# Half-height and half-width matmuls of the attention and scan products issued in pairs, on one Trainium2 core

## Chip, core and metric

The kernel runs on one core of a Trainium2 chip. The metric is the device time of one execution in microseconds (us). Products run on TensorE (PE; its weight loads are listed as PEld), elementwise work on VectorE (DVE), ScalarE (ACT) and GpSimd (POOL), and SyncE (SP) issues the transfers from HBM.

## What is computed

The reference chains three layers for 256 tokens of width 1024. The first has a context of 256 more tokens and mixes tokens in three ways: differential attention, a gated linear scan and neighbourhood attention. The other two are alike: latent attention (MLA), stick-breaking attention and a pooling mixer. Each layer ends in a mixture of 32 experts. Cut to what the change touches:

```python
# first layer: differential attention, 4 heads, two 64-wide score maps per head, values 128 wide
s = einsum('bqhmd,bkhmd->bhmqk', qb, kb) * 64 ** -0.5
p = softmax(s); d = p[:, :, 0] - lam * p[:, :, 1]; o = einsum('bhqk,bkhv->bqhv', d, vb)
# first layer: gated scan, 4 heads, 32-wide keys, 64-wide values, chunks of 64 tokens, both directions
o = einsum('bhts,bhsv->bhtv', a_intra, vc) + einsum('bhtd,bhdv->bhtv', qc * exp(b), s)
# first layer: neighbourhood attention, 4 heads of 64, keys of the grid and of the context
# second and third layer: MLA, 8 heads, 96-wide scores, 64-wide values; stick-breaking, 4 heads of 64
a = where(strict, exp(log_sigmoid(z) + between), 0); o = einsum('bhqk,bkhd->bqhd', a, v)
# each layer: out = x + mix @ w_out, then the experts
```

## The kernel before

One program does the three layers in order: `first_phase`, `moe_phase`, and twice `second_phase` with `moe_phase`. Weights come from HBM in units of 1 MB through a ring of 22 buffers in SBUF: a list of transfers in a fixed order, each issued by SP as soon as a buffer is released. All matmuls are on fp32 data except the projections and gathers, which use a high and a low fp32r part (`mm3`, L561). An fp32 matmul stands in the trace as two instructions (two passes) with a weight load each, so counts below are twice the number of calls.

The order of the engines' work is written by hand. In `first_phase` the scan's pieces lie between projections of the attention operands, in the order of `SEQ_A`: capital letters are projections, `k` is `g_kj` (64-row products of keys and values), `s` `g_state`, `t` `g_step` (chunk state times query, L1189), `i` `g_intra` (32-row scores of one head, L1176), `p` `g_pv` (64-column value products of one head, L1203). Two PSUM banks (`tr`) serve these, two more (`po`) collect the scan's output.

Attention runs as items in `run_items`, one item a step, four steps deep. At step s PE gets the scores of item s (DVE and ACT then do its softmax), the transposes of item s-2 (`fin`, followed by an ACT copy out of PSUM), a filler (projection, modulation, output product) and last the value product of item s-3. In the first layer there are eight differential items (two scores each, L1301) and eight neighbourhood items (one score, L1327). The second and third layers have 12 items in the order `ITEMS_B`: M for MLA (scores L2127, transposes L2148), S for stick-breaking (scores L2162 and L2163, a running sum in `fin`, L2180 to L2182). Their value products `pv` (L2114, L2116) fill 64 output rows for an even head and the other 64 for an odd one. A step's length is PE's own work, unless the softmax of an item isn't through.

Where a head uses only 64 of the 128 contraction rows (differential and neighbourhood scores, stick-breaking scores), the query was stored twice with the other 64 rows set to zero, and the matmul ran over all 128 rows:

```python
qaT = [bq.t[:, i * 1024:(i + 1) * 1024].rearrange("p (a t) -> p a t", a=4) for i in range(2)]
pool.memset(qaT[0][64:128], 0.0)
pool.memset(qaT[1][0:64], 0.0)
```

Of the kernel before, what the change touches and what calls it, by code (L numbers as in the profile page):

```python
# [27 lines left out]
SEQ_A = "A k0 B s0 s1 C k1 t0 D i1 E i2 t1 F i3 t2 p1 G i0 p2 p0 H t3 p3"  # L28
# [344 lines left out]
def hybrid_kernel(ctx: ExitStack, tc: tile.TileContext, A, out, dbg=None):  # L373
# [388 lines left out]
    def run_items(items, fillers, mode):  # L762
        n = len(items)
        for s in range(max(n + 3, len(fillers))):
            if mode and 2 <= s < n + 2:
                items[s - 2][2]()
            if s < n:
                items[s][0]()
                items[s][1]()
            if 2 <= s < n + 2:  # L770
                items[s - 2][3]()
            if not mode and 1 <= s <= n:
                items[s - 1][2]()
            if s < len(fillers):
                fillers[s]()
            if 3 <= s < n + 3:
                items[s - 3][4]()

    def first_phase():
        with ExitStack() as es:  # L780
# [321 lines left out]
            qaT = [bq.t[:, i * 1024:(i + 1) * 1024].rearrange("p (a t) -> p a t", a=4) for i in range(2)]  # L1102
            pool.memset(qaT[0][64:128], 0.0)
            pool.memset(qaT[1][0:64], 0.0)
# [3 lines left out]
            def rope(dsts, src, n, cs, sn):  # L1108
# [6 lines left out]
                m = 128 // len(dsts)  # L1115
                for i, d in enumerate(dsts):
                    hs = slice(m * i, m * i + m)
                    dve.tensor_add(d[hs], src[hs], sw[hs, 0:n])

            def ka_sink(i):  # L1120
                st = Unit()

                def sink(f, p):
# [4 lines left out]
                    if f == 1:  # L1128
                        rope([kaT[:, 2 * i:2 * i + 2, 0:256]], st.kr, 2, cosv, sinv)
                return sink  # L1130

            def qa_sink(i):
                def sink(f, p):
                    kr = wg.tile([128, 2, 256], F32, name="kr")
                    act.activation(kr.rearrange("p a t -> p (a t)"), p, AF.Copy, scale=0.125)
                    rope([q[:, 2 * i:2 * i + 2] for q in qaT], kr, 2, cosv, sinv)
# [14 lines left out]
            def g_kj(d):  # L1151
                names = ["kbT", "qbT", "kbt", "glT"]
                for par in range(2):
                    js = [j for j in ((0, 1, 2) if d == 0 else (1, 2, 3)) if j % 2 == par]
                    p = bank(ps, "tr")
                    for i, j in enumerate(js):
                        pe.matmul(p[:, i * 256:(i + 1) * 256], lhsT=k2[64 * par:64 * par + 64, d, j // 2],
                                  rhs=vbt[64 * par:64 * par + 64, j // 2], start=True, stop=True)
# [10 lines left out]
            def g_intra(h):  # L1169
                at[h] = quarters[0][h].rearrange("p (z f) -> p z f", z=4)  # L1170
                pool.memset(at[h], 0.0)
                pa = bank(ps, "tr")
                for a in range(2):
                    for d in range(2):
                        z = 2 * a + d
                        pe.matmul(pa[:, z * 128:(z + 1) * 128],  # L1176
                                  lhsT=k3[32 * h:32 * h + 32, d, a * 128:(a + 1) * 128],
                                  rhs=q3[32 * h:32 * h + 32, d, a * 128:(a + 1) * 128], start=True, stop=True)
                for a in range(2):
                    dve.copy_predicated(at[h][:, 2 * a:2 * a + 2], mfb,  # L1180
                                        pa[:, a * 256:(a + 1) * 256].rearrange("p (d t) -> p d t", d=2))
# [17 lines left out]
            def g_pv(h):  # L1199
                pr, o = h // 2, 64 * (h % 2)  # L1200
                for a in range(2):
                    for d in range(2):
                        pe.matmul(og[pr][o:o + 64, a * 128:(a + 1) * 128], lhsT=vbt[:, a, h * 64:(h + 1) * 64],  # L1203
                                  rhs=at[h][:, 2 * a + d], start=False, stop=(a == 1 and d == 1),
                                  skip_group_check=True)
# [35 lines left out]
            qnT = [wd.tile([128, 2, 256], F32, name=f"qnT{i}") for i in range(2)]  # L1241
            S.release(c1u)
            pool.memset(qnT[0][64:128], 0.0)
            pool.memset(qnT[1][0:64], 0.0)
# [4 lines left out]
            def values(h, dT, vals, w, kind):  # L1249
                hp, odd = h // 2, h % 2  # L1250
                if odd == 0:
                    hold.po = bank(ps, "po")
                po = hold.po
                o = po[:, odd * 256:odd * 256 + 256] if kind == "d" else po[64 * odd:64 * odd + 64, 0:256]
                for kt in range(4):
                    pe.matmul(o, lhsT=vals[:, kt, h * w:(h + 1) * w], rhs=dT[:, kt], start=(kt == 0), stop=(kt == 3))
                if odd == 0:
                    return
                if kind == "n":
                    act.activation(mixT[:, 6 + hp], po[:, 0:256], AF.Copy)  # L1260
# [60 lines left out]
            def near_item(h, qt):  # L1321
# [67 lines left out]
            def qn_sink(f, p):  # L1389
                for i in range(2):  # L1390
                    hs = slice(64 * i, 64 * i + 64)
                    act.activation(qnT[i].rearrange("p a t -> p (a t)")[hs], p[hs], AF.Copy, scale=0.125)
# [882 lines left out]
```

## Time and profile before

| | us |
|---|---|
| median of 3 runs (1385.88 to 1387.04) | 1386.26 |
| the profiled execution | 1387.48 |
| its span, first to last instruction | 1385.7 |
| PE busy in it | 1233.4 |
| DVE, ACT, POOL busy | 433.9, 342.9, 98.3 |
| mean granted clock of TensorE, share of 2.4 GHz | 0.958 |

Busy shares are means over stages with different limits. In the expert stages transfers run at 420 GB/s nearly throughout; in the mixing stages PE is busy nearly throughout and the transfers pause.

### The profile page before, as it was taken

The numbers are of one execution on the slowest core, as the hardware profiler recorded it, in microseconds if no ns is written. First come the engines' busy times: TensorE is split into PE (matmuls) and PEld (weight loads), VectorE is DVE, ScalarE is ACT, GpSimd is POOL, SyncE is SP. The second block draws the span as 40 slices with busy tenths as digits, with TensorE's granted clock in tenths as the row PEclk, the third lists the DMA queues.
The fourth block names the chain that finished last, engine by engine and source line by source line (L and its number), as shares of the span: only waits on it lengthen the run. The fifth ranks groups of instructions, "written<-read, shape, count | busy, mean of one in ns | idle before, by whom it ended". The sixth has DMA issues, their size and how long they took to land. (4 is left out here: it accounts for less than half of the span.)

```text
span 1385.7 us, 18830 instructions
## 1 busy us (share of the span) xinstructions
PE 1233.4 (89%) x7278; PEld 671.4 (48%) x7278; DVE 433.9 (31%) x1024; ACT 342.9 (25%) x709; POOL 98.3 (7%) x87
## 2 busy tenths in 40 slices
PE   5999999999976799998779998998778999999776
PEld 3788875464221154442258764443227866444222
DVE  5456362352111021221165434221005534422102
ACT  4432252221000010110146522211105642212102
POOL 1354100000000000000012100000000210000000
PEclk9999999999999899999899999999999999999998
DMA  9644417859999999999993548999999365899996
GB/s 360 220 180 167 183 61 313 359 207 394 420 422 421 421 421 422 421 420 420 421 413 133 203 173 339 421 421 420 421 420 375 122 273 196 349 420 421 421 421 246
DMA packets 64537, 459.40 MB, mean 332 GB/s; under 512 B 7408, under 2 KB 7728, under 8 KB 9904
## 3 DMA queue, kind: packets, MB, share of 16 engines
q1 hardware_dynamic: 64432, 458.04, 81.1%
q8 instruction: 62, 1.02, 0.3%
q14 instruction: 43, 0.35, 0.1%
HBM read 466.40 MB, written 1.05 MB: 337 GB/s over the span
## 5 line engine op out<-in xcount | busy, mean ns | idle before, releaser
L1696 PE MATMUL up<-ring,xg 128*32 128x512 f32 (+2 forms) x2016 | 381.5, 646 | 61.0 <-DMA ring<-in_gu_dram 33.3
L1696 PEld LDWEIGHTS up<-ring,xg 128*32 128x32 f32 (+2 forms) x2016 | 106.2, 127 | 305.8 <-issue 190.1
L1696 PE MATMUL mm<-ring,hdT 128*32 128x512 f32 (+2 forms) x1008 | 186.9, 620 | 27.0 <-DMA ring<-in_dn_dram 22.6
L561 PE MATMUL ps<-ring,ring 128*128 128x256 f32 (+1 forms) x960 | 146.6, 311 | 1.2 <-POOL ring L894 0.6
L561 PEld LDWEIGHTS ps<-ring,ring 128*128 128x128 f32 x960 | 131.3, 196 | 20.0 <-issue 5.8
L1712 DVE TENSOR_TENSOR hd<-hd,up 128x256 f32<-128x256 f32 (+1 forms) x32 | 16.7, 521 | 381.4 <-ACT hd L1711 359.1
L1696 PEld LDWEIGHTS mm<-ring,hdT 128*32 128x32 f32 (+2 forms) x1008 | 53.7, 124 | 138.8 <-issue 90.5
L1711 ACT ACTIVATE hd<-up 128x256 f32<-128x256 f32 (+1 forms) x32 | 14.9, 465 | 386.8 <-PE up L1696 386.8
L1512 PEld LDWEIGHTS mm<-P,ring 128*128 128x128 f32 x512 | 67.0, 200 | 12.0 <-issue 10.3
L1512 PE MATMUL mm<-P,ring 128*128 128x256 f32 x512 | 71.1, 296 | 0.6 <-DVE xg L1522 0.3
L596 PE MATMUL mm<-ring,ring 128*128 128x512 f32 (+1 forms) x192 | 64.1, 487 | 0.0
L1742 DVE SCALAR_TENSOR_TENSOR yl<-mm,gt,yh 128x512 fp32r<-128x512 f32 x40 | 30.0, 751 | 96.0 <-ACT yh L1741 96.0
L1741 ACT ACTIVATE yh<-mm,gt 128x512 fp32r<-128x512 f32 x40 | 27.5, 688 | 98.8 <-PE mm L1696 98.8
L1736 DVE SCALAR_TENSOR_TENSOR mm<-mm,gt,gmod 128x512 f32<-128x512 f32 x24 | 18.2, 759 | 98.3 <-PE mm L1696 98.3
L1738 ACT ACTIVATE yh<-mm 128x512 fp32r<-128x512 f32 x24 | 14.3, 597 | 139.1 <-DVE mm L1736 139.1
L1989 PE MATMUL ps<-ring,ring 128*128 128x256 f32 x384 | 48.7, 286 | 0.0
L1989 PEld LDWEIGHTS ps<-ring,ring 128*128 128x128 f32 x384 | 47.1, 192 | 0.7 <-ACT ring L1968 0.4
L596 PEld LDWEIGHTS mm<-ring,ring 128*128 128x128 f32 x192 | 35.8, 190 | 23.7 <-issue 21.5
L1958 POOL TENSOR_SCALAR ring<-ring,fr 128x1024 f32<-128x1024 f32 x2 | 5.7, 2852 | 420.2 <-DMA ring<-in_win_dram 420.2
L820 POOL TENSOR_TENSOR ring<-ring,ring 128x1024 fp32r<-128x1024 f32 x12 | 30.2, 2513 | 49.0 <-ACT ring L819 38.2
L1942 DVE TENSOR_TENSOR ring<-ring,ring 128x1024 fp32r<-128x1024 f32 x24 | 28.1, 1221 | 14.1 <-ACT ring L1938 14.0
L1750 PE MATMUL po<-yh,sm 128*128 128x512 f32 x64 | 28.4, 444 | 1.6 <-ACT yh L1738 1.4
(464 smaller groups left out, 1385.6 us busy)
## 6 DMA issues: line engine op xcount, KB each, us to landing
ring<-in_gu_dram SPq DMA_DIRECT2D x128, 1024.0 KB, 19.7
ring<-in_dn_dram SPq DMA_DIRECT2D x124, 1024.0 KB, 19.7
ring<-in_up_dram SPq DMA_DIRECT2D x120, 1024.0 KB, 19.2
ring<-in_wmod_dram SPq DMA_DIRECT2D x24, 1024.0 KB, 5.1
ring<-in_win_dram SPq DMA_DIRECT2D x24, 1024.0 KB, 11.3
ring<-in_wout_dram SPq DMA_DIRECT2D x12, 1024.0 KB, 18.3
ring<-in_c_dram SPq DMA_DIRECT2D x2, 896.0 KB, 14.0
ring<-in_wsm_dram SPq DMA_DIRECT2D x2, 784.0 KB, 14.5
```

Source lines behind the costliest of these rows:

```text
L561: pe.matmul(out, lhsT=a, rhs=b, start=first and i == 0, stop=last and i == 2, skip_group_check=True)
L596: pe.matmul(po, lhsT=O.mixT[:, s, a * 128:(a + 1) * 128], rhs=O.w[2 * c + s // 4][:, s % 4, sl.start - 512 * c:sl.stop - 512 * c], start=( ...
L820: (pool if q else dve).tensor_sub(lo[:, sl], u.t[:, sl], hi[:, sl].bitcast(F32))
L1512: pe.matmul(o, lhsT=xx[:, a, dt * 128:(dt + 1) * 128], rhs=P[:, a], start=(k == 0), stop=(k == 3))
L1696: pe.matmul(out[w * e:w * e + w], lhsT=x_of(w * e, w * e + w), rhs=wt, start=start, stop=stop)
L1712: dve.tensor_mul(hd, hd, pu[:, hid:uw])
L1736: dve.scalar_tensor_tensor(pd, pd, s.gt, gmod[:, hf * 512:(hf + 1) * 512], op0=OP.mult, op1=OP.mult)
L1741: act.activation(yh, pd, AF.Copy, scale=s.gt)
L1742: dve.scalar_tensor_tensor(yl, pd, s.gt, yh.bitcast(F32), op0=OP.mult, op1=OP.subtract)
L1750: pe.matmul(y[2 * a + hf], lhsT=s.sm[:, a * 128:(a + 1) * 128], rhs=s.y[hf][i], start=False, stop=True, skip_group_check=True)
L1942: dve.tensor_sub(lo[:, sl], u.t[:, sl], hi[:, sl])
L1989: pe.matmul(p[:, f * 256:(f + 1) * 256], lhsT=w[pw][:, dt, f * 128:(f + 1) * 128], rhs=hT[ph][:, dt], start=(i == 0 and f == 0 and dt == 0 ...
```

## The change

Scores with 64 contraction rows now run on the upper or the lower 64 rows alone, two of them one after the other in program order, one on either half; the zero halves, their memsets and the second copies go. `g_intra` takes two heads at once (row groups 32 and 64, then 96 and 0), `g_step` uses the half of the state that isn't zero, `g_pv` alternates two heads on the two column halves. The neighbourhood and MLA and stick-breaking value products of an even head wait for the odd one, and both are issued alternately. Neighbourhood and stick-breaking scores of an odd head are issued with those of the even one, a step earlier. Neighbourhood items are reordered so that the heads of a pair follow each other. In `run_items` the value products of item s-3 move from the end of the step to before the transposes of item s-2 and the filler. Core of the diff:

```diff
-SEQ_A = "A k0 B s0 s1 C k1 t0 D i1 E i2 t1 F i3 t2 p1 G i0 p2 p0 H t3 p3"
+SEQ_A = "A k0 B s0 s1 C k1 t0 D i0 E t1 F i1 t2 G p0 H t3 p1"
...
             if s < n:
                 items[s][0]()
                 items[s][1]()
+            if 3 <= s < n + 3:
+                items[s - 3][4]()
             if 2 <= s < n + 2:
                 items[s - 2][3]()
             if not mode and 1 <= s <= n:
                 items[s - 1][2]()
             if s < len(fillers):
                 fillers[s]()
-            if 3 <= s < n + 3:
-                items[s - 3][4]()
...
-            def rope(dsts, src, n, cs, sn):
+            def rope(dst, src, n, cs, sn):
...
-                for i, d in enumerate(dsts):
-                    hs = slice(m * i, m * i + m)
-                    dve.tensor_add(d[hs], src[hs], sw[hs, 0:n])
+                dve.tensor_add(dst, src, sw[:, 0:n])
...
-            def g_intra(h):
+            def g_intra(i):
+                hs = (1, 2) if i == 0 else (3, 0)
...
+                        for h, pa in zip(hs, pas):
+                            pe.matmul(pa[:, z * 128:(z + 1) * 128],
+                                      lhsT=k3[32 * h:32 * h + 32, d, a * 128:(a + 1) * 128],
+                                      rhs=q3[32 * h:32 * h + 32, d, a * 128:(a + 1) * 128], start=True, stop=True)
...
-                        pe.matmul(og[pr][:, j * 64:(j + 1) * 64], lhsT=st[d][:, pr * 128:(pr + 1) * 128],
-                                  rhs=q1[:, d, j * 64:(j + 1) * 64], start=first[pr], stop=False,
+                        hs = slice(64 * pr, 64 * pr + 64)
+                        pe.matmul(og[pr][:, j * 64:(j + 1) * 64], lhsT=st[d][hs, pr * 128:(pr + 1) * 128],
+                                  rhs=q1[hs, d, j * 64:(j + 1) * 64], start=first[pr], stop=False,
...
-            def g_pv(h):
-                pr, o = h // 2, 64 * (h % 2)
+            def g_pv(pr):
                 for a in range(2):
                     for d in range(2):
+                        for h in (2 * pr, 2 * pr + 1):
+                            o = 64 * (h % 2)
...
+                if kind == "n":
+                    if odd == 0:
+                        return
+                    po = bank(ps, "po")
+                    for kt in range(4):
+                        for m in range(2):
+                            j = 2 * hp + m
+                            pe.matmul(po[64 * m:64 * m + 64, 0:256], lhsT=vals[:, kt, j * w:(j + 1) * w],
+                                      rhs=dts[kind, j][:, kt], start=(kt == 0), stop=(kt == 3))
...
                     for m in range(2):
-                        pe.matmul(t.p[m], lhsT=qaT[m][:, h, qt * 128:(qt + 1) * 128], rhs=kaT[:, h], start=True,
+                        hs = slice(64 * m, 64 * m + 64)
+                        pe.matmul(t.p[m], lhsT=qaT[hs, h, qt * 128:(qt + 1) * 128], rhs=kaT[hs, h], start=True,
                                   stop=True)
...
-                    t.p = bank(ps)
-                    pe.matmul(t.p, lhsT=qnT[h % 2][:, hp, qt * 128:(qt + 1) * 128], rhs=knT[:, hp], start=True,
-                              stop=True)
+                    if h % 2 == 0:
+                        hold.p = [bank(ps), bank(ps)]
+                        for m in range(2):
+                            hs = slice(64 * m, 64 * m + 64)
+                            pe.matmul(hold.p[m], lhsT=qnT[hs, hp, qt * 128:(qt + 1) * 128], rhs=knT[hs, hp],
+                                      start=True, stop=True)
+                    t.p = hold.p[h % 2]
...
-            items += [near_item(h, q) for h in range(4) for q in range(2)]
+            items += [near_item(2 * g + m, q) for g in range(2) for q in range(2) for m in range(2)]
...
-            for i in range(2):
-                hs = slice(64 * i, 64 * i + 64)
-                act.activation(flat3(qbT[i])[hs], pqb[hs], AF.Copy, scale=0.125)
+            act.activation(flat3(qbT), pqb, AF.Copy, scale=0.125)
...
             def pv(h, slot, vals, pT, odd_done):
                 hp, odd = h // 2, h % 2
                 if odd == 0:
-                    hold.po = bank(ps, "po")
-                po = hold.po
...
+                    hold.pT = pT
+                    return
+                po = bank(ps, "po")
+                pair = ((0, hold.pT), (1, pT))
+                for m, v in pair:
+                    j = 64 * (2 * hp + m)
+                    pe.matmul(po[64 * m:64 * m + 64, 0:256], lhsT=vals[:, 0, j:j + 64], rhs=v[:, 0:256], start=True,
+                              stop=False)
...
+                    if h % 2 == 0:
+                        hold.p = [bank(ps), bank(ps)]
+                        for k0, n0, c0, n in ((0, 0, 0, 256), (128, 128, 256, 128)):
+                            for m in range(2):
+                                hs = slice(64 * m, 64 * m + 64)
+                                pe.matmul(hold.p[m][:, c0:c0 + n], lhsT=kbT[hs, hp, k0:k0 + 128],
+                                          rhs=qbT[hs, hp, n0:n0 + n], start=True, stop=True)
+                    t.p = hold.p[h % 2]
...
-                for g in (2 * gp, 2 * gp + 1):
+                for z, (c0, n) in enumerate(((0, 256), (256, 128))):
+                    for g in (2 * gp, 2 * gp + 1):
```

`g_kj` issues its three matmuls by position instead of by parity, the pooling product `pool_part` by source half instead of by group, and the copies `qn_sink` and `qaT` lose their second half in the same way as `qbT`.

## Rows read from the trace of the kernel before

**Rows 1.** The page: the transfer engines' busy tenths in 40 slices.

```profile
DMA  9644417859999999999993548999999365899996
```

**Rows 2.** Stretches: us, busy PE, PEld, DVE, ACT, POOL, clock, DMA share, GB/s.

```profile
95.00:160.00 65.00, 65.00 (x466) 55.23 (x465) 32.75 (x46) 15.91 (x24) 21.00 (x13) 1.00 0.41 157
160.00:217.00 57.00, 55.92 (x312) 42.59 (x313) 29.86 (x60) 25.22 (x54) 5.93 (x4) 1.00 0.24 86
217.00:260.00 43.00, 41.04 (x205) 20.23 (x198) 15.05 (x38) 16.41 (x37) 0.67 (x1) 0.96 1.01 421
752.00:802.00 50.00, 48.12 (x276) 36.36 (x275) 20.65 (x55) 24.17 (x70) 8.80 (x12) 0.97 0.56 219
```

**Rows 3.** PE's timeline in two windows of 0.3 us: start, us, instructions running there.

```profile
104.12 0.49 PE L1157 MATMUL tr<-ring,ring 64*128 64x256 f32 x2
...
780.96 0.44 PE L2201 MATMUL tr<-ring,ring 128*64 128x256 f32 x2
```

**Rows 4.** PE's timeline in the scan, 128 to 132 us.

```profile
128.69 1.15 PE L1176 MATMUL tr<-ring 32*128 32x128 f32 x8
129.77 1.10 PE L1189 MATMUL po<-ring,st 128*128 128x64 f32 x8
130.81 1.09 PE L1203 MATMUL po<-ring,ring 128*64 128x128 f32 x8
131.82 1.06 PE L957 MATMUL ps<-ring,ca 128*32 128x512 f32 x8
```

**Rows 5.** PE's timeline in the second layer's attention, 753 to 765 us.

```profile
753.24 0.89 PE L2127 MATMUL ps<-ring,ring 96*128 96x256 f32 x4 [0.67 <-ACT ring L2100]
753.89 4.61 PE L561 MATMUL ps<-ring,ring 128*128 128x256 f32 x24
758.33 0.59 PE L2162 MATMUL ps<-ring 128*128 128x256 f32 x2
...
758.98 0.49 PE L2148 MATMUL tr<-cm,e 128*128 128x128 f32 x3
759.23 3.12 PE L561 MATMUL ps<-ring,ring 128*128 128x256 f32 x24
...
762.84 0.49 PE L2148 MATMUL tr<-cm,e 128*128 128x128 f32 x3
763.26 0.65 PE L2114 MATMUL po<-pT,ring 128*64 128x256 f32 x2
...
764.06 0.92 PE L2127 MATMUL ps<-ring,ring 96*128 96x256 f32 x4
764.81 0.38 PE L2180 MATMUL tr<-sp,ring 128*128 128x256 f32 x1
```

**Rows 6.** PE's timeline around steps of the attention that have no filler.

```profile
174.43 0.66 PE L1282 MATMUL tr<-cm,pe 128*128 128x128 f32 x4 [0.64 <-DVE pe L1317]
...
180.41 1.88 PE L1301 MATMUL ps<-ring,ring 128*128 128x512 f32 x4
182.12 0.60 PE L1282 MATMUL tr<-cm,pe 128*128 128x128 f32 x4
...
791.68 0.52 PE L2148 MATMUL tr<-cm,e 128*128 128x128 f32 x3 [0.91 <-ACT pT L2150]
```

**Rows 7.** ACT's timeline in the same stages.

```profile
183.73 0.59 ACT L1285 ACTIVATE ring<-tr 128x512 f32<-128x512 f32 x1
...
735.12 1.20 ACT L2025 ACTIVATE ring<-ps 64x512 f32<-64x512 f32 x2 [4.05 <-PE ps L1989]
736.34 0.47 ACT L568 ACTIVATE rsq<-tr,epst 128x256 f32<-128x256 f32 x1
...
762.39 0.38 ACT L2216 ACTIVATE ring<-ps 128x256 f32<-128x256 f32 x1 [0.59 <-PE ps L561]
...
765.17 0.47 ACT L2150 ACTIVATE pT<-tr 128x384 f32<-128x384 f32 x1
791.06 0.47 ACT L2150 ACTIVATE pT<-tr 128x384 f32<-128x384 f32 x1
```

More of the change, by code (lines that the diff above doesn't have):

```diff
@@ L1128, in sink @@
                     if f == 1:
-                        rope([kaT[:, 2 * i:2 * i + 2, 0:256]], st.kr, 2, cosv, sinv)
+                        rope(kaT[:, 2 * i:2 * i + 2, 0:256], st.kr, 2, cosv, sinv)
                 return sink
@@ L1135, in sink @@
                     act.activation(kr.rearrange("p a t -> p (a t)"), p, AF.Copy, scale=0.125)
-                    rope([q[:, 2 * i:2 * i + 2] for q in qaT], kr, 2, cosv, sinv)
+                    rope(qaT[:, 2 * i:2 * i + 2], kr, 2, cosv, sinv)
                 return sink
@@ L1152, in g_kj @@
                 names = ["kbT", "qbT", "kbt", "glT"]
-                for par in range(2):
[L1154 to L1158, printed above, removed]
+                ps2 = [bank(ps, "tr") for _ in range(2)]
+                jss = [[j for j in ((0, 1, 2) if d == 0 else (1, 2, 3)) if j % 2 == par] for par in range(2)]
+                for i in range(2):
+                    for par in range(2):
+                        if i < len(jss[par]):
+                            j = jss[par][i]
+                            pe.matmul(ps2[par][:, i * 256:(i + 1) * 256], lhsT=k2[64 * par:64 * par + 64, d, j // 2],
+                                      rhs=vbt[64 * par:64 * par + 64, j // 2], start=True, stop=True)
+                for par in range(2):
+                    js, p = jss[par], ps2[par]
                     if len(js) == 1:
@@ L1167, in g_kj @@
                         dve.tensor_mul(kj[d, j], p[:, i * 256:(i + 1) * 256], bd)
-            def g_intra(h):
-                at[h] = quarters[0][h].rearrange("p (z f) -> p z f", z=4)
-                pool.memset(at[h], 0.0)
-                pa = bank(ps, "tr")
+            def g_intra(i):
+                hs = (1, 2) if i == 0 else (3, 0)
+                pas = []
+                for h in hs:
+                    at[h] = quarters[0][h].rearrange("p (z f) -> p z f", z=4)
+                    pool.memset(at[h], 0.0)
+                    pas.append(bank(ps, "tr"))
                 for a in range(2):
@@ L1175, in g_intra @@
                         z = 2 * a + d
[L1176 to L1181, printed above, removed]
+                        for h, pa in zip(hs, pas):
+                            pe.matmul(pa[:, z * 128:(z + 1) * 128],
+                                      lhsT=k3[32 * h:32 * h + 32, d, a * 128:(a + 1) * 128],
+                                      rhs=q3[32 * h:32 * h + 32, d, a * 128:(a + 1) * 128], start=True, stop=True)
+                for h, pa in zip(hs, pas):
+                    for a in range(2):
+                        dve.copy_predicated(at[h][:, 2 * a:2 * a + 2], mfb,
+                                            pa[:, a * 256:(a + 1) * 256].rearrange("p (d t) -> p d t", d=2))
             first = [True, True]
@@ L1240, in first_phase @@
             g2b = wk.tile([128, 1024], F32, name="g2b")
-            qnT = [wd.tile([128, 2, 256], F32, name=f"qnT{i}") for i in range(2)]
+            qnT = wd.tile([128, 2, 256], F32, name="qnT")
             S.release(c1u)
-            pool.memset(qnT[0][64:128], 0.0)
-            pool.memset(qnT[1][0:64], 0.0)
             hold = Unit()
@@ L2157, in stick_item @@
                 t = Unit()
-                q, hp = qbT[h % 2], h // 2
+                hp = h // 2
                 def score():
-                    p = t.p = bank(ps)
-                    pe.matmul(p[:, 0:256], lhsT=kbT[:, hp, 0:128], rhs=q[:, hp], start=True, stop=True)
-                    pe.matmul(p[:, 256:384], lhsT=kbT[:, hp, 128:256], rhs=q[:, hp, 128:256], start=True, stop=True)
+                    if h % 2 == 0:
[6 more added lines that the diff above has]
+                    t.p = hold.p[h % 2]
                 def soft():
```

48 lines of the change are left out of this document (18 added, 30 removed).

## Prediction

> **What bounds the kernel now.** I read the page first. Its row of transfer tenths [rows 1] shows two kinds of stage: runs of nines, where expert weights stream and nothing but bytes counts, and three dips, the mixing stages of the three layers. All edits lie in the dips. There PE is the busy engine [rows 2]: 65.00 of 65.00 us in the scan, 55.92 of 57.00 and 41.04 of 43.00 in the first layer's attention, 48.12 of 50.00 in the second layer's. No other engine passes half, except POOL's and DVE's bursts. The third layer repeats the second, so what I work out for one counts twice.
>
> Transfers hide nothing that is saved there. Their share is 0.41, 0.24 and 0.56 in three of the four stretches. In 217 to 260 it is 1.01: the ring refills there. But behind it the tenths fall to 5 and 4 again, so SP waits for buffers, which PE's progress releases. A microsecond off PE's chain should therefore be a microsecond off the end. The question is how much of PE's saved work becomes waiting.
>
> **Do pairs overlap?** The trace already holds two cases. `g_kj` issues a matmul on the upper and one on the lower 64 rows, and two run at once in the first window; two groups of `pool_part` on different column halves run at once in the second [rows 3]. So I price a pair at the time of one. Both edits to these two functions I therefore cost at nothing: the order changes, the overlap is there.
>
> **What a switch costs.** In [rows 5] three transposes (0.25 us, 758.98 to 759.23) and a score of four passes (0.65, 758.33 to 758.98) follow full-height work. With a 64-column value product between them, of the same four widths and so 0.65 too, the stretch from 762.84 to 764.81 takes 1.97. That is 0.42 over 0.25 + 0.65 + 0.65. I take 0.4 us for one trip into a half-size mode and back, for rows as for columns, since no row trip stands alone in these rows; its bounds are 0 and twice that. The Trainium skill, TensorEngine Tiling (Array Packing), section Key Properties, says that changing the tiling mode drains the engine, which speaks against this change, as it adds 16 such trips. The trace agrees in kind, with its 0.42; a sum that prices packing by the section Theoretical Speedup alone (up to twice) would leave the drain out and come 6.4 us lower.
>
> **Scan.** `g_intra`: four calls of 1.08 us (128.69 to 129.77) become two of the same length with two heads each: 2.16 saved. `g_step`: four of 1.04 (129.77 to 130.81) with eight passes each, half of them now beside the other half: 0.45 each, 1.8. `g_pv`: four of 1.01 (130.81 to 131.82) become two: 2.0 [rows 4]. Sum 5.96, less 0.1 because two of the four stood side by side: **5.9**. PE waits for nothing here [rows 2], and `SEQ_A` leaves a projection between every product and the DVE work that it needs, so I expect no new wait. DVE's shorter `rope` and POOL's memsets are worth nothing, as PE covers them. If pairs with 32 rows don't overlap, 2.16 go.
>
> **First layer's attention, PE's work.** Two scores take 1.71 (180.41 to 182.12) [rows 6]; as a pair 0.86 + 0.4. Eight differential items save 8 x 0.46 = 3.7. Eight neighbourhood scores, 6.9, become four pairs of 1.26: 1.85. Their value products are eight passes of 256, 0.215 each by [rows 5], so 1.73 + 0.4; four calls become two: 4.25. Sum 9.8.
>
> **What is late next.** Value products now come ahead of the filler, so PE meets the copy by ACT one step after the transposes, with only a score between. Where the step before had no filler, the softmax of DVE and ACT isn't through. PE already waits 0.64 us there for DVE [rows 6]. By walking the steps I find four such spots. The scores of items 1 and 2 gain 0.9, but their softmax starts only 0.46 earlier, so the wait grows to 1.1 or more (I count 1.7, the two reductions being in line on DVE). At the first value product PE arrives at about 182.9, while the copy that starts at 183.73 [rows 7] moves to 183.3 and ends 0.59 later: 1.0. The norm of heads 2 and 3 waits for a square behind ACT's exponentials: 1.0. The first neighbourhood pair waits for two softmaxes in a row: 2.0, taken as twice the one before. Together 5.7 in place of the 3.0 that PE idles now (1.08 + 1.96, [rows 2]): **9.8 - 2.7 = 7.1**. Bounds: 4 if the waits are twice as long, 9.8 if none is new.
>
> **Second and third layer, each.** Twelve value products of 0.65 + 0.4 become six: 6.3. Four stick-breaking scores of 0.65 become two pairs of 1.05: 0.5. Both pooling products lose the column-mode neighbour they had, 0.8 lost. Work saved: 6.0. New waits: the second value product now stands before projection u0. ACT is held by the copy behind v1 (762.39, [rows 7]), then has three activations of stick-breaking, then the copy at 765.17 to 765.64; that lies in the same place, but PE is there at 763.6. Wait 1.65. The pair of stick-breaking heads waits 0.85 and 0.65 for the exponential. The pair at the end of the scores waits, as PE does now at 791.68 with 0.91 [rows 6], for ACT's copy of 791.06 [rows 7], now 1.85 since less work lies ahead. Score M4 loses the product that stood between it and DVE's copy of its PSUM bank, 0.5. Sum 5.5, in place of 1.2 (0.91 and a few short ones): 4.3 of the 6.0 go, 1.7 stay. One thing is added: ACT's two half copies of `qbT`, 1.20 us, become one of 0.6. The next activation starts at once at 736.34 [rows 7], and the norm, rope and scores hang on it: 0.6. **2.3 each, 4.6** for both. Bounds 0.6 and 6.6.
>
> **Clock.** In [rows 2] the granted clock is 0.96 in 217 to 260 and 0.97 in 752 to 802. That is 3.4 and 3.0 us at 1.2 GHz instead of 2.4. In the second case 24 matmuls took 4.44 (753.89 to 758.33), where the next 24 took about 3.0 [rows 5]; it followed a wait of 0.67 for the scores at 753.24. So a spell costs 1.4 us, and I allow one more of them for about 14 new waits.
>
> **Sum.** 5.9 + 7.1 + 4.6 - 1.4 = 16.2. The profiled execution took 1387.48; 1387.5 - 16.2 = 1371.3. The median of the runs lies 1.2 under it, so I predict **1370 us**.
>
> **The rivals.** A change under 0.2% (2.8 us) can't be told from none here.
> - *The forecast*, 1370, within 1366 to 1375: chance 0.52.
> - *Switches are hidden* behind the next weight load: 16 trips of 0.4 more, 1363.8. For it: an engine that loads ahead. Against: the 0.42 of [rows 5] was not hidden. 0.10.
> - *Waits eat all of the attention's gain*; scan and `qbT` remain: 5.9 + 1.2 = 7.1, so 1387.5 - 7.1 - 1.2 = 1379.2. For it: 70% of the second layer's gain goes already by my walk. 0.18.
> - *Row halves don't overlap*, so half of the change does nothing. Lost: `g_intra` 2.16, `g_step` 1.8, 12 score pairs of 0.86 (10.3), stick-breaking 2.6: 16.9, which is 1387. Against: the first of [rows 3]. 0.07.
> - *Transfers take back the first layer's gain* in 217 to 260: 13.0 lost, 1383. Against: the dip behind it in [rows 1]. 0.05.
> - *Slower: the clock.* If each of the 14 new waits brings a spell of 3.4 us at half clock, of pure PE work, it costs 1.7: 23.8 in all, 1387.5 - 17.6 + 23.8 - 1.2 = 1392.5. It turns slower once a wait costs over (17.6 + 2.8) / 14 = 1.46. For it: the spells now also stand behind waits. Against: one in either of two stretches of 43 and 50 us, in which PE idles 1.96 and 1.88 [rows 2]. 0.08. The Trainium skill, TensorE: Matmul & The Clock Gate, section HAM oscillation, describes this loss, waits between bursts putting the clock back to half. The trace agrees with it at 753.89, not at 791.68, where PE waited longer: the 0.97 of that stretch has room for the one spell alone.
>
> **Numbers.** Faster by over 0.2% means under 1383.5: the first three and two fifths of the transfers' case, 0.82, which I round to 0.81; same 0.11; slower 0.08. The range leaves out the clock, the row halves and a little below the hidden switches: 1361 to 1384.
>
> **What would show it.** Pairs of L1301 and L2162 with two instructions in flight; four scores' passes in about 0.86; L1176 with 16 passes in 1.08; about 6 us less from 95 us to the end of the scan, 13 to the end of the first attention, 2 each later; PE idle in front of L2114 for ACT L2150, and PE's busy time lower by 20 us or more. Wrong would be: one instruction in flight in the scores, clock under 0.9 in a mixing stage, or a transfer at the end of the waits before 270 us.

## Result and the profile after

The changed kernel took 1371.2 us in the median of its runs (1369.2 to 1375.1), the kernel before 1386.3: a ratio of 0.989, interval 0.987 to 0.992. The forecast was 1370, within 1361 to 1384. Timed again beside the experiments it took 1373.0, with 0.990 (0.989 to 0.992). The profiled execution took 1371.44 us, the one before 1387.48.

From the page of the changed kernel: PE's busy time, the clock that it was granted and the transfers' tenths in 40 slices.

```profile
PE 1205.1 (88%) x7278; PEld 652.5 (48%) x7278; DVE 431.1 (31%) x1022; ACT 340.4 (25%) x706; POOL 93.0 (7%) x79
...
PEclk9999999999998899999989998999999999999998
DMA  9645508969999999999993647999998365999995
```

The transfers look as in [rows 1]: three dips at the mixing stages, nines between. PE's busy time is 28.3 us lower; 24.4 of it lie in the stretches below, with the third layer's attention, which repeats the second's.

To compare equal work I cut both traces at the same instructions: scan (first state product to the norm behind it), first attention (first score to the first output product of the stage behind it), and second layer's attention likewise. Columns: us, busy PE, PEld, DVE, ACT, POOL, clock, DMA share, GB/s. The kernel before, then the changed one:

```profile
95.36:156.39 61.03, 61.03 (x439) 51.82 (x438) 32.75 (x46) 13.99 (x21) 21.00 (x13) 1.00 0.38 142
...
163.00:260.70 97.70, 94.66 (x488) 60.04 (x487) 44.90 (x97) 41.62 (x91) 6.60 (x5) 0.98 0.58 233
751.68:802.18 50.50, 48.62 (x277) 36.66 (x278) 20.97 (x55) 24.48 (x71) 9.12 (x12) 0.97 0.56 219
```

```profile
94.18:149.46 55.28, 55.28 (x440) 46.61 (x439) 30.86 (x44) 13.99 (x21) 20.73 (x13) 1.00 0.42 157
...
156.15:251.41 95.26, 86.57 (x488) 55.19 (x487) 44.42 (x97) 40.56 (x90) 5.58 (x3) 0.95 0.54 213
741.11:787.77 46.66, 43.34 (x276) 32.27 (x277) 20.81 (x55) 24.40 (x71) 9.14 (x12) 1.00 0.59 235
```

The scan gained 5.75 us, and PE stayed busy throughout. The second layer's attention gained 3.84 (the third's the same). The first attention gained only 2.44, although PE worked 8.1 us less: its idle time, us less busy PE, grew from 3.04 to 8.69, and the mean clock fell from 0.98 to 0.95.

PE's timeline of the changed kernel at some pairs (start, us, instructions):

```profile
111.09 1.16 PE L1179 MATMUL tr<-ring 32*128 32x128 f32 x16
112.18 5.73 PE L561 MATMUL ps<-ring,ring 128*128 128x512 f32 x24
...
156.15 1.13 PE L1314 MATMUL ps<-ring,ring 64*128 64x512 f32 x4
157.21 5.74 PE L561 MATMUL ps<-ring,ring 128*128 128x512 f32 x24
...
746.36 0.92 PE L2181 MATMUL ps<-ring 64*128 64x256 f32 x8
747.22 0.55 PE L2163 MATMUL tr<-cm,e 128*128 128x128 f32 x3
...
751.56 0.65 PE L2128 MATMUL po<-pT,ring 128*64 128x256 f32 x2
753.02 0.43 PE L2128 MATMUL po<-pT,ring 128*64 128x256 f32 x1 [0.82 <-ACT pT L2165]
...
766.52 0.65 PE L2128 MATMUL po<-pT,ring 128*64 128x256 f32 x4
...
767.32 0.70 PE L2200 MATMUL tr<-sp,ring 128*128 128x256 f32 x2
```

Pairs overlap in all three kinds: sixteen 32-row passes take 1.09 us, where eight took 1.08 [rows 4]. From a pair's start to the next instruction's start, differential scores take 1.06, stick-breaking scores 0.86, latent-attention values 0.80. One full-size product takes 0.86, 0.65 and 0.65 there. So of a trip into a half-size mode and back, 0.15 to 0.21 lie between a pair and what follows it; what the neighbouring instructions lose isn't in these numbers (see the last experiment with scores apart). The rows at 751.56 and 753.02 show a pair that does not overlap: the even head goes first, alone, and the odd head waits for ACT's copy. Of the six value pairs of this layer two run as the one at 766.52 does; four are split.

What PE waited for in the first attention of the changed kernel (us in total, times, longest):

```profile
PE tr L1294 <- DVE pe L1330: 2.1, 1, 2.1
PE tr L1294 <- DVE t L1391: 1.8, 1, 1.8
PE tr L1368 <- ACT rs__1646 L568: 1.4, 1, 1.4
PE po L1270 <- ACT ring L1297: 1.2, 1, 1.2
PE tr L1368 <- DVE mr L963: 0.9, 1, 0.9
PE tr L1279 <- ACT sqd L1275: 0.6, 1, 0.6
PE tr L596 <- ACT ring L1264: 0.5, 1, 0.5
...
```

Only the 1.2 and the 0.6 stand in front of a value product or its norm. Four of the others stand in front of transposes, of the softmaxes' results (L1294) and of the modulation rows (L1368); the last stands in front of the output product (L596).

In the second layer, likewise:

```profile
PE po L2128 <- ACT pT L2165: 2.1, 2, 1.3
PE ps L2142 <- ACT ring L2111: 0.7, 1, 0.7
PE ps L2142 <- DVE ring L2097: 0.7, 1, 0.7
...
```

The first row is the forecast's wait of value products for ACT's copy; the two of 0.7 were there before [rows 5].

**The clock.** In the traces the granted clock falls to half in spells of 3.4, 6.8 or 10.2 us. Behind the wait of 2.09 us for DVE in the first attention, the 24 passes of a projection took 7.35 us from 167.37 on; elsewhere 5.73. Here is the clock (the column behind POOL's) of a stretch with that wait and of the one behind it, first in the profiled execution of the changed kernel, then in the same kernel profiled once more:

```profile
164.88:168.30 3.42, 1.34 (x8) 1.22 (x9) 3.28 (x9) 2.10 (x7) 0.28 (x1) 1.00 0.58 175
168.30:171.70 3.40, 3.40 (x10) 2.62 (x9) 1.31 (x3) 1.17 (x4) 0.00 (x0) 0.50 0.32 133
```

```profile
165.20:168.60 3.40, 1.31 (x10) 1.16 (x9) 3.26 (x9) 2.07 (x7) 0.31 (x1) 1.00 0.53 176
168.60:172.00 3.40, 3.40 (x17) 2.79 (x16) 1.36 (x3) 1.23 (x4) 0.00 (x0) 1.00 0.32 133
```

PE had waited the same 2.09 us in both executions, and only in one was it put to 1.2 GHz. So one profile's time holds an element of chance, and I list for every kernel the first attention's time, its idle time and its us at half clock. Passes run half as fast there, so a spell costs about half its length (1.62 us for the 24 passes above); the last column takes half of it off.

| kernel | us | PE idle | at half clock | us at full clock |
|---|---|---|---|---|
| before | 97.70 | 3.04 | 3.4 | 96.0 |
| scan alone | 96.04 | 3.05 | 0 | 96.0 |
| order alone | 100.94 | 4.55 | 6.8 | 97.5 |
| changed | 95.26 | 8.69 | 10.2 | 90.2 |
| changed, profiled again | 93.68 | 8.68 | 6.8 | 90.3 |
| changed, old order | 90.21 | 7.92 | 0 | 90.2 |
| changed, scores apart | 93.80 | 5.55 | 3.4 | 92.1 |
| changed, filled waits | 92.95 | 4.26 | 3.4 | 91.2 |
| before, finer fillers | 92.71 | 0.47 | 0 | 92.7 |
| changed, finer fillers | 83.33 | 0.85 | 0 | 83.3 |
| changed, finer fillers, scores apart | 87.46 | 0.85 | 0 | 87.5 |

Kernels with the same instructions there (rows 1 and 2; 4 and 5) agree within 0.1 in the last column, though up to 1.7 apart in the first.

### The profile page after: what moved, and what is told of

Its sections match the earlier page's. It is cut to its first block, busy times and chain, and to the rows that moved or that the text cites. A ratio compares the mean times of both kernels' runs of the same rounds, so it can differ in the third digit from the quotient of the medians.

```text
span 1369.6 us, 18802 instructions
## 1 busy us (share of the span) xinstructions
PE 1205.1 (88%) x7278; PEld 652.5 (48%) x7278; DVE 431.1 (31%) x1022; ACT 340.4 (25%) x706; POOL 93.0 (7%) x79
## 2 busy tenths in 40 slices
DMA packets 64536, 459.39 MB, mean 335 GB/s; under 512 B 7408, under 2 KB 7728, under 8 KB 9904
## 5 line engine op out<-in xcount | busy, mean ns | idle before, releaser
L1711 PE MATMUL up<-ring,xg 128*32 128x512 f32 (+2 forms) x2016 | 372.7, 625 | 62.9 <-DMA ring<-in_gu_dram 35.6
L596 PE MATMUL mm<-ring,ring 128*128 128x512 f32 (+1 forms) x192 | 64.1, 487 | 0.0
L596 PEld LDWEIGHTS mm<-ring,ring 128*128 128x128 f32 x192 | 35.8, 190 | 23.7 <-issue 21.5
```

Source lines behind the costliest of these rows:

```text
L596: pe.matmul(po, lhsT=O.mixT[:, s, a * 128:(a + 1) * 128], rhs=O.w[2 * c + s // 4][:, s % 4, sl.start - 512 * c:sl.stop - 512 * c], start=( ...
L1711: pe.matmul(out[w * e:w * e + w], lhsT=x_of(w * e, w * e + w), rhs=wt, start=start, stop=stop)
```

## Experiments

My theory T1 at the start: pairing saves what it was priced at, but value products moved ahead of transposes and filler expose ACT's copies, and half-clock spells follow these waits. Rivals: the chain of softmaxes sets the pace whatever the order; spells fall by chance; transfers take the gain back.

**The scan alone**, in the kernel before:

```diff
-SEQ_A = "A k0 B s0 s1 C k1 t0 D i1 E i2 t1 F i3 t2 p1 G i0 p2 p0 H t3 p3"
+SEQ_A = "A k0 B s0 s1 C k1 t0 D i0 E t1 F i1 t2 G p0 H t3 p1"
# and g_kj, g_intra, g_step, g_pv as in the change
```

> The kernel before with the edits to the scan alone (g_kj, g_intra, g_step, g_pv and the scan's order). Theory T1, that pairs save PE's time as they were priced and that the rest of the change's gain is partly lost again in the first layer's attention: 5.8 us less at the scan's end, which is what the changed kernel's trace showed there, and this stays to the end: 1380.5. Rival A, that what the scan saves is given back behind it by transfers, since the ring refills: under 2.8 us in all, 1384 to 1386, with the output product of the first layer starting less than 3 us earlier. Rival B, that part of the 5.8 us belongs to the shorter rope and the dropped memsets, which this kernel keeps: 3 to 5 us, 1381.5 to 1383.

1379.5 us, ratio 0.994 (0.992 to 0.996). Its trace has the scan at the changed kernel's length:

```profile
94.37:149.66 55.29, 55.29 (x439) 46.61 (x438) 31.91 (x46) 13.99 (x21) 21.12 (x13) 1.00 0.41 158
```

55.29 against 55.28, with the longer rope and the memsets still in it, so B falls, and A with it: 8 us are kept in the medians (1387.5 for the kernel before beside it), of which 5.74 are the scan's. The rest lies within the spread of the runs (1383.3 to 1391.8 for the kernel before); no run here tells where it comes from.

**The order alone**, in the kernel before:

```diff
+            if 3 <= s < n + 3:
+                items[s - 3][4]()
             if 2 <= s < n + 2:
                 items[s - 2][3]()
...
-            if 3 <= s < n + 3:
-                items[s - 3][4]()
```

> The kernel before with one edit: in every step of the three attentions the value product stands ahead of the transposes and of the filler, as in the changed kernel; nothing is paired. T1, that this order exposes ACT's copy of the transposes in steps without a filler: 2 to 4 us slower in the first attention, with waits of some 1 us in front of value products (DVE and ACT in front of them), 1 to 2 us slower in the second and third each; 1390 to 1394. Rival C, that the softmax chain sets the pace and the order only moves a wait from one instruction to another: within 1 us in each attention, 1385 to 1388.

1393.8 us, ratio 1.0042 (1.0027 to 1.0056): slower, as T1 says. What PE waits for there, in the first attention:

```profile
PE po L1256 <- ACT ring L1285: 1.6, 2, 1.2
...
PE tr L1351 <- ACT rs__1654 L568: 0.9, 1, 0.9
```

The stretch of its second layer's attention:

```profile
754.61:805.76 51.15, 47.42 (x276) 35.37 (x277) 21.09 (x55) 24.73 (x71) 9.15 (x12) 1.00 0.55 221
```

The same stretch in the scan-alone kernel, with the old order and no spell either:

```profile
746.35:795.36 49.01, 47.13 (x277) 35.18 (x278) 20.97 (x55) 24.46 (x71) 9.11 (x12) 1.00 0.57 223
```

At full clock the first attention loses 1.5 (97.5 against 96.0) and the second layer's 2.14 (51.15 against 49.01), the third's the same: 5.8 in all. Without pairs the order costs in all what T1 gave it, but less than its 2 to 4 in the first attention and more than its 1 to 2 in each later one.

**The old order in the changed kernel**, first attention only (there with one value product left ahead); the second and third layer keep the new order, so for them nothing is tested.

```diff
-            if 3 <= s < n + 3:
+            if s - 3 in early:
                 items[s - 3][4]()
             if 2 <= s < n + 2:
                 items[s - 2][3]()
...
+            if 3 <= s < n + 3 and s - 3 not in early:
+                items[s - 3][4]()
# first layer: early = (11,); second and third: all steps
```

> The changed kernel, with the value product last in each step of the first attention again, as before the change (one step, whose buffer would be overwritten, keeps the new order; the second and third layer keep it too). T1: the waits in front of value products (1.2, 1.2 and 0.3 us for ACT in the changed kernel) go, and with them some of the half-clock spells behind them: the first attention, which gained 2.4 us, gains 4 to 7; 1366 to 1369.5. Rival C, that the softmax of DVE and ACT sets the pace there whatever the order: waits in front of transposes take their place, the first attention stays within 1 us, 1370 to 1372.

1369.0 us, ratio 0.988 (0.984 to 0.992). (The changed kernel has one wait of 1.2 us in front of a value product, not the two that are named there.) By the time alone T1 would stand. The trace says otherwise; its longest waits in the first attention:

```profile
PE tr L1296 <- DVE pe L1332: 3.5, 2, 2.1
PE tr L1296 <- DVE t L1393: 1.1, 1, 1.1
PE po L1264 <- ACT ring L1299: 0.9, 1, 0.9
```

The waits went from value products to transposes, as rival C has it: 7.92 us idle against 8.69, and 90.2 us at full clock in both. The 5 us that this profile gained in the stretch are spells that it did not have, and 2.7 of them went again behind it: from the output product to the first expert it took 43.5 us with 10.2 at half clock, the changed kernel 40.8 with 3.4. So T1's first half falls for the changed kernel: with pairs and with these fillers the softmaxes set the pace in the first attention, and the order is free.

**Differential scores apart**, in the changed kernel:

```diff
-                        pe.matmul(t.p[m], lhsT=qaT[hs, h, qt * 128:(qt + 1) * 128], rhs=kaT[hs, h], start=True,
+                        pe.matmul(t.p[m], lhsT=qaT[m][:, h, qt * 128:(qt + 1) * 128], rhs=kaT[:, h], start=True,
# and the two zero-padded copies of the queries as before
```

> The changed kernel, with the differential attention's two scores per item on all 128 rows again, one after the other, from two zero-padded copies of the queries as before (rope writes both copies, two memsets come back). If PE sets the pace in these eight steps, 8 x 0.65 = 5.2 us are lost by the 1.06 us that a pair took against 1.71 for two. T1, that in these steps the softmax of DVE and ACT sets the pace in the changed kernel (it saved 2.9 us of PE's work there and lost 0.64 us of time): 0 to 1.5 us slower, 1371 to 1373, with PE idling less. Rival D, PE sets the pace and the loss lies in half-clock spells alone: 3.5 to 5.2 us slower, 1374.7 to 1376.4.

1373.6 us, ratio 0.990 (0.987 to 0.993): the same as the changed kernel's. The stretch of the differential scores (first of them to the first neighbourhood score), there and in the changed kernel:

```profile
156.92:198.03 41.11, 39.59 (x181) 27.06 (x179) 27.02 (x53) 21.36 (x46) 4.94 (x2) 1.00 0.28 103
```

```profile
156.15:197.44 41.29, 36.64 (x180) 25.02 (x179) 26.55 (x53) 20.70 (x46) 4.91 (x2) 0.96 0.29 102
```

With one spell of 3.4 us taken off (1.7), the pairs leave PE 34.9 us of work in place of 39.6 and 4.65 us of idle time in place of 1.5: two thirds of what these eight pairs save is waited away, 1.5 us stay. That is T1's case (0 to 1.5), not D's.

**The changed kernel again**, unchanged:

> The changed kernel once more, for the spread of its time and for the place of its half-clock spells. If the spells follow from the waits alone, the profile shows them again where it did (10 us at half clock in the first attention, in front of 95 us from its first score to the output product) and 1371 again. If they fall by chance on one wait or another, the first attention takes another time, between 90.5 (no spell, 95.3 less half of 10) and 97, with the same idle time of 8.7 within 0.3, and what it gains or loses is not found again in the other stages: 1368 to 1375 over the runs.

1373.0 us (1371.1 to 1377.3). The idle time is the same again, 8.68; the spells are not, 6.8 us at 196 and 234 us in place of 10.2 at 168 and 233. So the waits alone don't settle where the spells fall.

**Waits filled**, in the changed kernel, with products that nobody reads:

```diff
+            def idle(p, n, x):
+                for _ in range(n):
+                    pe.matmul(p, lhsT=ones, rhs=x, start=True, stop=True)
             def finish_item(h, qt, e, kind):
                 p = bank(ps, "tr")
+                idle(p, {("d", 0, 0): 2, ("n", 1, 1): 2}.get((kind, h, qt), 0), (knT if kind == "n" else kaT)[:, 0])
...
+                idle(po, 1 if h == 0 else 0, kaT[:, 0])
```

> The changed kernel with five products that nobody reads (128 rows, 512 columns, 0.86 us each) in front of three of its longest waits in the first attention: two before the transposes that waited 2.09 us, one before the value product that waited 1.16, two before the transposes that waited 1.79. They add no result and take PE's waiting time. If the waits put the clock down, the spells behind them go or shorten: 3 to 4 us less in the first attention, 1367 to 1369. If the spells fall where they fall by chance, the same time within the spread, 1370 to 1373. If the products delay the chain more than they fill, some 1 to 2 us more: 1372 to 1374.

1369.3 us, ratio 0.988 (0.987 to 0.990). The products cost 1.0 us of delay at full clock, 3.4 us were at half clock in place of 10.2 and 6.8, and the median is 3.7 under the changed kernel's beside it and 1.9 under its first timing. The intervals still touch, so this alone settles nothing.

**Finer fillers.** If the softmaxes set the pace, PE must get its other work where they are late. In the changed kernel with the old order, the projections are cut in halves and dealt over the steps that had none:

```diff
-FILL_A = "k0 . k1 . . q . r1 va+vb+m1 m1 . m6+r2+rel sl sb . o+o4 o6 o7 ."
+FILL_A = "k0 k1 K1 q Q va VA r1+vb VB m1 m2 m2+rel m3+mr r2 sl sb+o+o4 o6 o7 ."
```

> The changed kernel with the value product last in the first attention again (one step keeps the new order), and its fillers cut finer and dealt out: the projections of the neighbourhood keys, queries and values in halves in steps 1 to 8, the eight modulation products in 1, 2, 2, 3 in steps 9 to 12 where six stood in one step, so that no step up to 17 is without one. T1, that PE's waits there come from steps without a filler: idle time in the first attention from 7.9 us to 3 to 5, so 86 to 88 us where the old order alone took 90.2 and the change 95.3: 1362 to 1366. Rival C, that the chain of softmaxes sets the pace: idle time stays over 7 us and the time with it, 1367 to 1370.

1363.4 us, ratio 0.983 (0.982 to 0.985). The differential items and the whole first attention:

```profile
157.62:201.34 43.72, 43.72 (x252) 31.92 (x251) 27.37 (x53) 21.08 (x47) 4.97 (x2) 1.00 0.27 97
157.62:240.95 83.33, 82.48 (x487) 52.02 (x487) 45.06 (x97) 40.37 (x90) 5.64 (x3) 1.00 0.57 223
```

0.85 us idle and no spell: 6.9 us better at full clock than the change. C, with its 7 us of idle time, falls; T1 had 3 to 5 and was too careful. The softmaxes set the pace in the changed kernel only because the fillers stood elsewhere.

**Finer fillers in the kernel before:**

> The kernel before with the finer fillers of the kernel above and nothing else. T1: it has 3.0 us of waits in the first attention, about 2 of them at steps without a filler, so 0 to 2.5 us less, 1384 to 1387. Rival E, that the finer dealing is worth as much by itself as with pairs (4 us and more): 1380 to 1383.

1384.0 us, ratio 0.997 (0.996 to 0.999). Its first attention:

```profile
163.22:255.93 92.71, 92.24 (x489) 59.45 (x488) 45.70 (x97) 41.77 (x91) 6.58 (x5) 1.00 0.57 227
```

It falls between the two expectations: 3.3 us at full clock, 2.6 of them idle time. From 92.7 to 83.3 the pairs are then worth 9.4 us, and PE's work falls by 9.8 (92.24 to 82.48), as the forecast had it.

**Finer fillers, scores apart:**

> The kernel with the finer fillers and the old order in the first attention (1363.4), its differential scores on all 128 rows again as before the change. With the changed kernel's own fillers the same edit had moved PE's waits from 4.65 to 1.5 us and left the time of these eight steps where it was, half-clock spells aside. Now PE waits for nothing in these steps. T1, pairing is worth what it saves of PE's work only where PE waits for nothing: 8 x (1.71 - 1.06) = 5.2 us slower, in the first eight steps alone: 1367.5 to 1369.5. Rival C, the softmaxes still set the pace of these steps: 0 to 1.5 slower, 1362.5 to 1365.

1368.3 us, ratio 0.987 (0.984 to 0.989), 4.9 over the kernel with pairs. The same eight items:

```profile
155.95:203.79 47.84, 47.84 (x252) 35.76 (x250) 27.73 (x53) 21.87 (x47) 4.93 (x2) 1.00 0.25 89
```

47.84 against 43.72: the pairs that were worth 1.5 us in the changed kernel are worth 4.1 where PE waits for nothing. That is 0.52 a pair. T1 had 0.65, from 1.71 for two scores and 1.06 for a pair, and left out what the neighbours lose. PE's timeline around one pair, and around the same two scores apart:

```profile
174.23 3.11 PE L561 MATMUL ps<-ring,ring 128*128 128x256 f32 x24
177.27 1.13 PE L1327 MATMUL ps<-ring,ring 64*128 64x512 f32 x4
178.33 0.66 PE L1307 MATMUL tr<-cm,pe 128*128 128x128 f32 x4
```

```profile
174.62 3.12 PE L561 MATMUL ps<-ring,ring 128*128 128x256 f32 x24
177.58 1.88 PE L1331 MATMUL ps<-ring,ring 128*128 128x512 f32 x4
179.30 0.60 PE L1312 MATMUL tr<-cm,pe 128*128 128x128 f32 x4
```

From start to start, the projection ahead of the pair takes 3.04 in place of 2.96, and the pair 1.06 in place of 1.72. A pair at the time of one score would save 0.86; it saves 0.52, so the trip into the 64-row mode and back costs 0.34, of which 0.20 lie between the pair and what follows.

**Finer fillers in the later layers too:**

```diff
-FILL_B = ". v0 v1 . u0 . . u1 p0 f p1 f+o o2 o4+o5 o6"
+FILL_B = ". v0 v1 V1 u0 U0 u1 U1 p0 f . p1+o f+o2 o4+o5 o6"
```

> The kernel with the finer fillers, and the same done to the second and third layer's attention: its value and pooling projections cut in halves where a step was empty (steps 2 to 7), the second pooling product a step later, so that a filler stands ahead of the value products that waited 0.82 and 1.29 us. T1: idle time in each of these two attentions from 3.31 to 1 to 2 us, 46.66 to 44.4 to 45.5 us, and with 1363.4 as the start 1358 to 1361. Rival F, that PE's wait only moves on to the products with the triangle, which wait for the exponentials of stick-breaking: 46 us and more in each, 1362 to 1364.5.

1357.1 us, ratio 0.979 (0.976 to 0.981). Second layer's attention:

```profile
731.23:775.39 44.16, 42.12 (x276) 32.09 (x277) 20.84 (x55) 24.22 (x71) 9.14 (x12) 1.00 0.61 249
```

46.66 became 44.16, and the third's as much: 5.0 of the 6.3 us between the medians. Idle time fell by 1.3 and PE's work by 1.2: three of the six value pairs now overlap whole and a fourth in part, where two did. F falls.

**Routing filled.** In every kernel so far PE waits 2.5 to 2.8 us for DVE ahead of the product that places tokens. In the kernel with finer fillers in the first layer:

```diff
+        for _ in range(3):
+            pe.matmul(pls[1][:, 64:448], lhsT=ones, rhs=xT[:, 1, 0:3].rearrange("p k t -> p (k t)"), start=True,
+                      stop=True)
         place(1)
```

> The kernel with the finer fillers, and in each layer's routing three products that nobody reads (384 columns, 0.65 us each) in front of the placing product, which waits 2.5 us for DVE in every kernel so far. They add no result. If such waits put the clock down, the spells behind them (10.2, 3.4 and 6.8 us at half clock in the three stages from the output product to the first expert) go or shorten, 1.7 us for each 3.4: 1357 to 1361. If spells fall where they fall by chance, or the products come too early or late in the wait to change anything, the same: 1362 to 1365. If they delay the placing product, 1 to 2 us slower.

1357.1 us, ratio 0.979 (0.977 to 0.981), where the same kernel without the products, timed in an earlier round, had 0.983 (0.982 to 0.985). The placing product (L715) in the first layer without and with them, and then the clock behind it without and with them:

```profile
276.43 0.64 PE L715 MATMUL mm<-mk,cm 128*128 128x32 f32 x2 [2.47 <-DVE rpm L718]
```

```profile
273.79 2.10 PE L755 MATMUL up<-xT,ones 128*128 128x384 f32 x6
276.44 0.41 PE L715 MATMUL mm<-mk,cm 128*128 128x32 f32 x2 [0.54 <-DVE rpm L718]
```

```profile
276.40:283.20 6.80, 6.38 (x31) 6.18 (x32) 2.08 (x7) 1.13 (x2) 0.00 (x0) 0.50 0.82 308
```

```profile
276.40:283.20 6.80, 6.00 (x44) 5.06 (x46) 2.64 (x9) 2.26 (x4) 0.00 (x0) 1.00 0.81 308
```

The placing product starts within 0.01 us of where it did, and what follows runs at 2.4 GHz in place of 1.2. From the output product to the first expert the three layers took 41.5, 38.1 and 38.1 us, in place of 43.5, 39.8 and 40.9: 6.3 us, as much as the medians differ.

**All together,** with one more such product in the first layer, between the two halves of the sum that gives its expert scores. With it the scores came out different, and so the experts that are fetched (449.98 MB in place of 459.39) and the result: this kernel computes something else. Its time of 1332.7 us stands beside no other, and its trace is read by stretches alone.

> The kernel with finer fillers in all three attentions (1357.1), with the three unread products ahead of the placing product in each layer's routing, and one more in the first layer ahead of the expert scores that waited 0.86 us for DVE's copy, where a half-clock spell of 3.4 us had stayed. T1, filled waits keep the clock up: 6.3 us off, as the same products took from 1363.4, and 1.7 for the last spell: 1349 to 1352, with no spell between the first layer's output product and its first expert. If the one spell was chance, no gain from the last product and up to 0.7 us of delay: 1350.5 to 1352.5. If the 6.3 us were chance, 1355 to 1358.

The first layer's stretch took 39.8 us with no spell, against 41.5 with three products. But in the later two layers a spell of 3.4 us stood behind the filled wait again, 39.8 us each. The clock there in the second layer:

```profile
796.80:800.20 3.40, 3.40 (x19) 3.40 (x18) 0.97 (x2) 1.17 (x3) 0.00 (x0) 0.50 1.00 422
```

So filling lessens the spells and doesn't bar them: over the three stages 3.4 and 6.8 us at half clock in the two kernels with it, 10.2 to 20.5 in the twelve profiles without. That is one profile for either kernel.

## Why the prediction was right

**Overlap**: right, for 32 and 64 rows and for 64 columns.

**The trip at 0.4**: near for rows, 0.34 by the eight differential pairs where PE waits for nothing (4.1 us saved; the forecast had 3.7). For columns the 0.80 of a value pair shows 0.15 behind the pair, and no run shows the whole. The 0.42 of [rows 5] was a single column product between transposes and scores of 96 rows, so more than the mode's change may lie in it. The rival of hidden switches falls for rows. Its price was wrong too: the sum also credits 14 fewer column trips (5.6) and charges four more at the pooling products (1.6), so with free switches it would come 2.4 lower, not 6.4. The Trainium skill, TensorEngine Tiling (Array Packing), section Key Properties, says that changing the tiling mode drains the engine; the 0.34 agree in kind.

**Scan, 5.9**: 5.75 measured, by [rows 4]'s terms, with no new wait.

**First attention, 7.1**: 5.8 at full clock, and 9.3 us gained by its end where 13 were forecast. The step that was off is "what is late next": work fell by more than 9.8 (96.0 - 3.0 = 93.0 to 90.2 - 8.7 = 81.5, so 11.5; with the finer fillers it fell by 9.8, and no run splits the difference), but waits are 8.7, not 5.7. Right were the transposes of step 2 (1.7, measured 2.1), the first value product (1.0, 1.2) and the norm (1.0, 0.6). Missed were the modulation transposes behind ACT's roots (1.4) and a wait of 1.8 for DVE in front of a later step's transposes; the 2.0 at the first neighbourhood pair did not come. The reason given, the value product ahead of the filler, holds for the kernel without pairs and not for this one, as the old order showed. The rival that waits eat all of the gain had a part of the truth: two thirds of the work that the differential pairs save went so.

**Later layers, 2.3 each**: 2.35 at full clock in the attention (49.01 to 46.66) and 0.73 ahead of it for `qbT` and the half-copies (forecast 0.6), 3.1 together. Two sizes were off and nearly cancel: work fell by 3.8, not 6.0, and idle time rose by 1.4, not 4.3. A pair's even head starts alone while the odd head's copy is late (751.56 above), so part of the wait is worked through and the pair does not overlap. And the 6.3 for six fewer value products counted 0.4 for each trip; at the 0.80 measured they are worth 4.8.

**Clock, 1.4 lost**: the first attention lost 3.4 by it in one profile and 1.7 in the other; the kernel before had lost 1.5 in each later attention (50.50 against 49.01), where the changed one had no spell. From the output product to the first expert the second and third layer took 40.7 us each with 6.8 at half clock, before 39.5 and 39.4 with 3.4: 2.5 lost, which the forecast did not name.

**Sum, and luck**: without the clock it is 5.75 + 5.8 + 2 x 3.1 = 17.7 against the forecast's 17.6, but only because the first attention's 1.3 too much and the later layers' 1.6 too little cancel. The two profiled executions differ by 16.0, against 16.2; 1.2 of that was gained ahead of the scan (its start at 94.18 us, before 95.36), where no pair stands. There the first spell lasted 3.4 us in place of 6.8. Over all fourteen profiles the first product of `g_kj` starts at 87.4 to 87.9 us in the six with 3.4, at 88.1 to 89.0 in the eight with 6.8. So the mechanism was right in kind, and part of the number's fit is luck.

**Transfers**: not at the end of any wait there, as forecast; what the mixing stages saved was kept through the experts.

## What to carry to other kernels

Pairing half-used products saves their full time, less the trip into the mode and back, only where PE waits for nothing: find who is late at the step where PE becomes faster, and deal other work to that step. When single profiles differ by a few us, compare idle time and us at half clock ahead of time itself, or a change of order gets praised for what the clock did. A wait on TensorE that can't be removed can be worth filling with products that nobody reads, if they end before it does.

## What the hardware showed that I had not expected

The same wait of 2.09 us brought a half-clock spell in one execution and none in another of the same kernel. That is a likely reason why runs of one kernel spread by some 6 us (1369.2 to 1375.1 for the changed one); no run here tells it from others. Spells stood behind short waits: of 2.1 and 2.5 us for DVE, and of 1.4 us for ACT (the spell at 196 us in the changed kernel's second profile). The Trainium skill, TensorE: Matmul & The Clock Gate, section HAM oscillation, tells of such losses with waits of 3 to 5 us for transfers in every round; the traces agree in kind, and show it for shorter and single waits, on other engines.

A matmul on fp32 data stands as two instructions in the trace, one behind the other, and pairs issued in the order A, B overlap all the same: both instructions of A beside both of B, 1.06 us for four that take 0.43 each in turn.
